# A hybrid retention and SSD block: two buffers for the tile of decays, six instead of seven for the weights' high parts

## The chip, the cores and the metric

The kernel runs on one core of a Trainium2 chip. The metric is the device time of one execution in microseconds (us). A difference below 0.2% of the time, about 5.5 us here, cannot be told from no change.

## The reference

One layer of a streaming encoder on 512 positions, model width 2048, all in float32:

```python
h = rmsnorm(x, norm1_w)
proj = einsum('bsd,de->bse', h, w_in)            # 2048 -> 22592 columns
q, k, v, g_ret, z, xbc, dt_raw, gate_r, gate_s = split(proj)
y_r = retention(q, k, v, positions) * silu(g_ret)      # 8 heads x 256, rotary, group norm
y_s = ssd(xbc, dt_raw, ...)                            # 64 heads x 64, state 128, chunked scan
y_s = rmsnorm(y_s * silu(z), ssd_norm_w)
merged = sigmoid(gate_r) * (y_r @ w_br_ret) + sigmoid(gate_s) * (y_s @ w_br_ssd)
x = rmsnorm(x + merged @ w_out, norm_f_w)
```

In the SSD branch each head has a scalar decay per position. Inside a chunk, the output is `(C B^T * decay) x`, where `decay[l, s] = exp(acum[l] - acum[s])` for `l >= s`. The tile of decays that this document is about holds these exponentials.

## The kernel before

**Units.** Every projection is cut into units of 256 output columns. A unit multiplies eight slices of 256 input rows (k = 0 to 7) with its weights. It uses Strassen's scheme with seven products for most units (`SEVEN`) and plain products for some (`FOUR`). Each product is three matmuls, since weights and operands are split into a high part and a low part of reduced precision: L202 (weights' high part times operands' high part), L203 (high times low) and L204 (low times high). The results stand in four PSUM banks, `pb0` to `pb3`.

**The weights' path.** For a pair of k, SP loads the weights into `wf` (L216, `FB` = 3 buffers). DVE forms the Strassen sums in place (L219, L221, L222). Then `split` makes the two parts for each k: ACT casts `wf` into `whi` (L150, `HB` = 7 buffers), and DVE subtracts that from `wf` into `wlo` (L151, `LB` = 6 buffers). A buffer of `whi` comes free after the last L203 that reads it, one of `wlo` after the last L204. The products of k = 0 to 4 are issued k by k, those of the last three k bank by bank, so the last three `whi` and `wlo` are held until a unit's end. After a unit its banks are evicted: L255 on ACT and L256 to L259 on DVE (L250 to L252 for plain units).

**The stages.** Retention (8 heads of four units), SSD (8 groups), the two branch projections, and the output projection. A group of SSD has a unit for B and C; then twice a unit for x, a unit for z and the work on two blocks of 128 features (a block is two heads); and units of the merge gates between them.

**A feature block.** SP loads the cumulated decays into `L` (L642, 512 KB, from a tensor in DRAM). ACT makes eight Relu steps of 128x128 (L646) and one Exp of 128x1024 (L648, ahead of which a table load stands when the last function was of another table, as SiLU and sigmoid are). DVE multiplies the result by `CB` (L649). PE then multiplies with it (L653, eight in the program, of which the trace shows sixteen). `L` had one buffer: the next block's load waits until the L653 of this block are done. Beside this runs the state's part: transposes (L620), `xd` on DVE (L622), `xl` on POOL (L625), L629 on PE, `S` on ACT and DVE (L632, L636), and L657 on PE. L659 to L662 on DVE put the block's output together.

**The order.** The program is written in the order of the code, and the framework's scheduler sets each engine's order from it, by priorities and by what its own model of the time says is ready. Each engine, and SP's queue of loads, then works strictly in that order. Another number of buffers gives another order on every engine.

Of the kernel before, what the change touches and what calls it, by code (L numbers as in the profile page):

```python
# [8 lines left out]
F32 = mybir.dt.float32  # L9
# [7 lines left out]
P = 128  # L17
T = 512
TB = T // P
# [80 lines left out]
          (((2, 0, 1, 6), (2, 0, 3, 2), (2, 1, 0, 6), (2, 1, 2, 2)),))  # L100
NP = KD // 2
LAST = 3
FB, HB, LB = 3, 7, 6
FORM_POOL = (1, 2, 3, 4, 5, 6, 7)
X_POOL = (2, 3, 4, 5, 6, 7)
PLAIN2 = (0, 7)
# [23 lines left out]
def hybrid_block(tc, A, out):  # L130
# [15 lines left out]
    def att_tile():  # L146
        return att.tile([P, T], F32, name="att")
# [409 lines left out]
    with tc.tile_pool(name="ssd", bufs=1) as sp:  # L557
# [30 lines left out]
        for g in range(NG):  # L588
# [14 lines left out]
            for jj in range(2):  # L603
# [5 lines left out]
                for e in range(2):  # L609
                    j = j0 + e  # L610
                    h0 = 2 * j
                    hs = slice(h0, h0 + 2)
                    y = xs[e]
                    E = sp.tile([P, T - P], F32, name="E")
                    for i in range(2):
                        SP.dma_start(out=E[i * 64:(i + 1) * 64, :], in_=E_d[h0 + i, P:].partition_broadcast(64))

                    ps = att_tile()
                    for c in range(TB):
                        PE.transpose(ps[:, c * P:(c + 1) * P], y[:, c * P:(c + 1) * P], ident)  # L620
                    xd = sp.tile([P, TB, 2, 64], F32, name="xd")
                    DVE.tensor_tensor(xd, ps.rearrange("p (c i d) -> p c i d", c=TB, i=2),  # L622
                                      dt[:, :, hs, None].to_broadcast([P, TB, 2, 64]), op=ALU.mult)
                    xl = sp.tile([P, TB - 1, 2, 64], F32, name="xl")
                    POOL.tensor_tensor(xl, xd[:, :TB - 1], tail[:, :TB - 1, hs, None].to_broadcast([P, TB - 1, 2, 64]),  # L625
                                       op=ALU.mult)
                    ps = att_tile()
                    for c in range(TB - 1):
                        PE.matmul(ps[:, c * P:(c + 1) * P], Bk[:, c, :], xl[:, c].rearrange("p i d -> p (i d)"),  # L629
                                  start=True, stop=True)  # L630
                    S = sp.tile([P, TB - 1, P], F32, name="S")
                    ACT.copy(S[:, 0, :], ps[:, :P])  # L632
                    for c in range(1, TB - 1):
                        for i in range(2):
                            d = slice(i * 64, (i + 1) * 64)
                            DVE.scalar_tensor_tensor(S[:, c, d], S[:, c - 1, d], cd[:, c, h0 + i:h0 + i + 1],  # L636
                                                     ps[:, c * P + i * 64:c * P + (i + 1) * 64],
                                                     op0=ALU.mult, op1=ALU.add)
                    pi = att_tile()

                    L = sp.tile([P, 2, TB, P], F32, name="L")
                    SP.dma_start(out=L.rearrange("p i c l -> p i (c l)"),  # L642
                                 in_=A_d[hs, :].partition_broadcast(P))
                    for i in range(2):
                        for c in range(TB):
                            ACT.activation(L[:, i, c, :], L[:, i, c, :], AF.Relu, scale=-1.0,  # L646
                                           bias=At[:, c, h0 + i:h0 + i + 1])
                    ACT.activation(L, L, AF.Exp, scale=-1.0)  # L648
                    DVE.tensor_tensor(L, L, CB[:, None].to_broadcast([P, 2, TB, P]), op=ALU.mult)  # L649

                    for c in range(TB):
                        for i in range(2):
                            PE.matmul(pi[i * 64:(i + 1) * 64, c * P:(c + 1) * P], xd[:, c, i, :], L[:, i, c, :],  # L653
                                      start=True, stop=True)
                    pe = att_tile()
                    for c in range(1, TB):
                        PE.matmul(pe[:, c * P:(c + 1) * P], S[:, c - 1, :], Ct[:, c * P:(c + 1) * P],  # L657
                                  start=True, stop=True)
                    DVE.scalar_tensor_tensor(y, y, dsk[:, j:j + 1], pi, op0=ALU.mult, op1=ALU.add)  # L659
                    DVE.tensor_tensor(E, pe[:, P:], E, op=ALU.mult)  # L660
                    DVE.tensor_tensor(y[:, P:], y[:, P:], E, op=ALU.add)
                    DVE.tensor_tensor(y, y, sz[e], op=ALU.mult)  # L662
                    if j == 0:
                        ACT.activation(sq, y, AF.Square)
                    else:
                        ACT.activation(sz[e], y, AF.Square)
                        POOL.tensor_tensor(sq, sq, sz[e], op=ALU.add)
                    ACT.activation(y, y, AF.Identity, scale=sn[:, j:j + 1])
                    ACT.dma_start(out=ys_d[j * P:(j + 1) * P, :], in_=y)
# [155 lines left out]
```

## Time and profile before

| | |
|---|---|
| median of 3 runs | 2768.67 us (2764.48 to 2770.89) |
| the profiled execution's own time | 2775.27 us |
| its span, first to last instruction | 2772.7 us, granted TensorE clock 0.992 |
| PE busy | 2701.6 us (97%) |
| DVE busy | 2389.5 us (86%) |
| ACT busy | 1343.8 us (48%) |
| retention / SSD / what follows | about 0 to 808, 808 to 2040, 2040 to 2773 us |

Busy time is counted by engine; PE counts matmuls, PEld the loading of their stationary operand, which overlaps. A wait is named as "engine and line that waited <- engine and line that ended the wait: us in total, times, longest us". Each engine waits in its own order, so a wait also holds back all that stands behind the instruction.

### The profile page before, as it was taken

To read this page: it belongs to the slowest core of one execution; us is meant where nothing else is said; L and a number is where in the kernel's file an instruction comes from. 1 tells how busy PE (TensorE), PEld (TensorE's weight loads), DVE (VectorE), ACT (ScalarE), POOL (GpSimd) and SP (SyncE) were. 2 spreads that over 40 slices of the span, in tenths; PEclk is the share of its full clock that TensorE was granted. 3 is DMA by queue.
4 is the path that set the end of the run, shared out by engine and by line. 5 is a ranking of instruction groups with operands and counts; after the bars stand their busy time and mean duration, and the time that the engine had idled before them with its cause. 6 is when DMAs were issued, how large, how long until landed. Compare 5 with 4: busy or idle time off the path is not lost.

```text
span 2772.7 us, 52195 instructions
## 1 busy us (share of the span) xinstructions
PE 2701.6 (97%) x20508; PEld 2567.9 (93%) x20508; DVE 2389.5 (86%) x3750; ACT 1343.8 (48%) x1884; POOL 268.3 (10%) x206
## 2 busy tenths in 40 slices
PE   7999999999999999999999999999999999999898
PEld 3899999999999999999999999999979989899798
DVE  8998888888869888988889899898989797888997
ACT  4344333333345565555565565565553343433453
POOL 4000000000000000000000000000020020121321
PEclk9999999999999999999999999999999999999999
DMA  3333333333333444343344434344365454556634
GB/s 125 99 103 103 97 111 104 103 92 103 103 112 120 128 128 129 113 125 122 123 128 130 133 115 126 117 126 130 125 193 167 157 186 136 165 184 198 218 113 137
DMA packets 339765, 362.46 MB, mean 131 GB/s; under 512 B 25152, under 2 KB 297792, under 8 KB 339520
## 3 DMA queue, kind: packets, MB, share of 16 engines
q1 hardware_dynamic: 319280, 325.31, 38.5%
q10 hardware_dynamic: 20240, 33.82, 3.3%
q8 instruction: 160, 2.62, 0.4%
q14 instruction: 85, 0.70, 0.1%
HBM read 321.56 MB, written 37.49 MB: 129 GB/s over the span
## 4 chain that ended last, share of the span: by engine, by line
PE 79%; DVE 10%; DMA 5%; issue 3%; POOL 1%; ACT 1%; SPq 1%; DVEq 0%; POOLq 0%; ACTq 0%
PE pb L204 21%; PE pb L203 21%; PE pb L202 21%; DVE wlo L151 3%; PE att L202 3%; PE att L204 3%; PE att L203 3%; DMA wf<-in_w_in_dram 3%; PE att L536 1%; PE att L521 1%; PE att L653 1%; DVE wf L219 1%; DMA wf<-in_w_br_ssd_dram 1%; PE att L657 1%; PE pb L120 1%
## 5 line engine op out<-in xcount | busy, mean ns | idle before, releaser
L203 PE MATMUL pb<-hl,whi 128*128 128x256 f32 (+1 forms) x5464 | 1599.5, 294 | 12.9 <-DVE hl L120 8.5
L202 PE MATMUL pb<-hh,whi 128*128 128x256 f32 (+1 forms) x5464 | 1597.7, 295 | 14.5 <-ACT hh L150 7.8
L204 PE MATMUL pb<-hh,wlo 128*128 128x256 f32 (+1 forms) x5464 | 1589.2, 294 | 5.1 <-DVE wlo L151 5.0
L150 ACT CAST whi<-wf 128x896 fp32r<-128x896 f32 (+1 forms) x968 | 819.6, 886 | 913.6 <-PE pb L203 367.2
L202 PEld LDWEIGHTS pb<-hh,whi 128*128 128x128 f32 x5464 | 1045.2, 192 | 40.3 <-ACT hh L150 8.9
L203 PEld LDWEIGHTS pb<-hl,whi 128*128 128x128 f32 x5464 | 1047.9, 192 | 35.9 <-DVE hl L120 10.2
L204 PEld LDWEIGHTS pb<-hh,wlo 128*128 128x128 f32 x5464 | 1041.7, 192 | 28.2 <-DVE wlo L151 7.1
L151 DVE TENSOR_TENSOR wlo<-wf,whi 128x896 fp32r<-128x896 f32 (+1 forms) x968 | 1005.1, 1051 | 56.3 <-ACT whi L150 32.1
L219 DVE TENSOR_TENSOR wf<-wf 128x512 f32<-128x512 f32 x404 | 289.9, 718 | 176.9 <-DMA wf<-in_w_in_dram 133.2
L202 PE MATMUL att<-hh,whi 128*128 128x256 f32 (+1 forms) x768 | 227.1, 297 | 3.0 <-ACT whi L150 3.0
L203 PE MATMUL att<-hl,whi 128*128 128x256 f32 (+1 forms) x768 | 226.7, 297 | 0.0
L204 PE MATMUL att<-hh,wlo 128*128 128x256 f32 (+1 forms) x768 | 222.8, 297 | 2.1 <-DVE wlo L151 2.1
L222 DVE TENSOR_TENSOR wf<-wf 128x256 f32<-128x256 f32 x404 | 179.9, 446 | 3.2
L221 DVE TENSOR_TENSOR wf<-wf 128x256 f32<-128x256 f32 x404 | 171.9, 426 | 3.5
L202 PEld LDWEIGHTS att<-hh,whi 128*128 128x128 f32 x768 | 147.4, 192 | 7.8 <-ACT whi L150 3.9
L204 PEld LDWEIGHTS att<-hh,wlo 128*128 128x128 f32 x768 | 144.8, 191 | 7.2 <-DVE wlo L151 3.1
L203 PEld LDWEIGHTS att<-hl,whi 128*128 128x128 f32 x768 | 147.5, 192 | 3.9
L625 POOL TENSOR_TENSOR xl<-xd,sst 128x384 f32<-128x384 f32 x32 | 35.1, 1097 | 848.7 <-DVE xd L622 791.1
L646 ACT ACTIVATE L<-L,sst 128x128 f32<-128x128 f32 x256 | 78.5, 389 | 29.7 <-DMA L<-A_d 29.7
L542 POOL TENSOR_TENSOR rs<-rs,mhalf 128x1 f32<-128x1 f32 x32 | 23.8, 750 | 712.9 <-DVE rs L541 678.8
L255 ACT COPY o<-pb 128x256 f32<-128x256 f32 x89 | 32.7, 367 | 117.9 <-PE pb L204 110.8
L256 DVE TENSOR_TENSOR o<-pb,o 128x512 f32<-128x512 f32 x89 | 60.8, 683 | 31.4 <-PE pb L204 30.8
(230 smaller groups left out, 2099.1 us busy)
## 6 DMA issues: line engine op xcount, KB each, us to landing
wf<-in_w_in_dram SPq DMA_DIRECT2D x640, 256.0 KB, 3.1
wf<-in_w_br_ssd_dram SPq DMA_DIRECT2D x128, 256.0 KB, 3.6
wf<-in_w_out_dram SPq DMA_DIRECT2D x72, 256.0 KB, 3.2
wf<-in_w_in_dram SPq DMA_DIRECT2D x128, 128.0 KB, 2.6
L<-A_d SPq DMA_DIRECT2D x32, 512.0 KB, 3.7
wf<-in_w_br_ret_dram SPq DMA_DIRECT2D x64, 256.0 KB, 3.5
ys_d<-B ACTq DMA_DIRECT2D x32, 256.0 KB, 2.2
E<-E_d SPq DMA_DIRECT2D x64, 96.0 KB, 3.4
```

Of the source, the lines that this page charges most:

```text
L150: ACT.copy(dst_hi, src)
L151: DVE.tensor_tensor(dst_lo, src, dst_hi.bitcast(F32), op=ALU.subtract)
L202: PE.matmul(o, wh, xh, start=b not in started, stop=False, skip_group_check=True)
L203: PE.matmul(o, wh, xl, start=False, stop=False, skip_group_check=True)
L204: PE.matmul(o, wl, xh, start=False, stop=(k == NP - 1), skip_group_check=True)
L219: DVE.tensor_tensor(f2[:, :, 4:6, :], f2[:, :, 1:3, :], f2[:, :, 0:1, :].to_broadcast([P, 2, 2, P]), op=ALU.subtract)
L221: DVE.tensor_tensor(f2[:, :, 0, :], f2[:, :, 2, :], f2[:, :, 4, :], op=ALU.add)
L222: DVE.tensor_tensor(f2[:, :, 6, :], f2[:, :, 3, :], f2[:, :, 0, :], op=ALU.subtract)
L255: ACT.copy(p1, pt[0][:, 0, :])
L256: DVE.tensor_tensor(o[:, 1:3, :], pt[1], p1[:, None, :].to_broadcast([P, 2, 256]), op=ALU.add)
L625: POOL.tensor_tensor(xl, xd[:, :TB - 1], tail[:, :TB - 1, hs, None].to_broadcast([P, TB - 1, 2, 64]), op=ALU.mult)
L646: ACT.activation(L[:, i, c, :], L[:, i, c, :], AF.Relu, scale=-1.0, bias=At[:, c, h0 + i:h0 + i + 1])
```

## The change

The pool of the decays' tile gets two buffers, and the pool of the weights' high parts loses one. Nothing is computed differently, and the instructions are the same but for the table loads that the new order needs (58 on ACT instead of 70: at L648 17 instead of 30, at L579 17 instead of 16).

```diff
-FB, HB, LB = 3, 7, 6
+FB, HB, LB = 3, 6, 6
...
-                    L = sp.tile([P, 2, TB, P], F32, name="L")
+                    L = sp.tile([P, 2, TB, P], F32, name="L", bufs=2)
                     SP.dma_start(out=L.rearrange("p i c l -> p i (c l)"),
                                  in_=A_d[hs, :].partition_broadcast(P))
```

The scheduler makes another order of this on every engine. Three places show it.

PE, SSD's fifth group, around the L653 of the first pair's second block, before (`pb_16478` to `pb_16480` are banks of the unit that runs beside it; `hh_266`, `hh_277`, `hh_288` are the operands of its k = 5, 6, 7):

```order
L202 MATMUL pb_16480<-hh_266,whi 128x256
L653 MATMUL att<-L,xd 64x128 x8
L657 MATMUL att<-A_8595,S 128x128 x2
L203 MATMUL pb_16480<-hl_284,whi 128x256
L204 MATMUL pb_16480<-hh_266,wlo 128x256
L202 MATMUL pb_16480<-hh_266,whi 128x256
L203 MATMUL pb_16480<-hl_284,whi 128x256
L204 MATMUL pb_16480<-hh_266,wlo 128x256
L202 MATMUL pb_16480<-hh_277,whi 128x256
L657 MATMUL att<-A_8595,S 128x128
```

The same place now:

```order
L202 MATMUL pb_16478<-hh_266,whi 128x256
L629 MATMUL att<-xl,A_8595 128x128 x3
L653 MATMUL att<-L,xd 64x128 x8
L203 MATMUL pb_16478<-hl_284,whi 128x256
L204 MATMUL pb_16478<-hh_266,wlo 128x256
L202 MATMUL pb_16477<-hh_277,whi 128x256
L203 MATMUL pb_16477<-hl_290,whi 128x256
L204 MATMUL pb_16477<-hh_277,wlo 128x256
L202 MATMUL pb_16478<-hh_277,whi 128x256
```

The second block's L653 moved up, to right behind its L629; its three L657 no longer stand close behind the L653 but further down, with products between them.

ACT, the same group, from the first pair's second block to the next block, before:

```order
L255 COPY o<-pb_16477 128x256
L669 DMA ys_d<-B_8596 128x512
L150 CAST whi<-wf 128x896 x3
L646 ACTIVATE L<-L,sst 128x128 x8
L584 ACT_TABLE_LOAD
L584 ACTIVATE o<-o 128x512 x2
L648 ACT_TABLE_LOAD
L648 ACTIVATE L<-L 128x1024
```

And now:

```order
L255 COPY o<-pb_16477 128x256
L646 ACTIVATE L<-L,sst 128x128 x8
L150 CAST whi<-wf 128x896
L648 ACTIVATE L<-L 128x1024
L150 CAST whi<-wf 128x896 x2
L584 ACT_TABLE_LOAD
L584 ACTIVATE o<-o 128x512 x2
```

The decays here are those of the next pair's first block before, and of the next pair's second block now; the Exp comes ahead of the gates' sigmoid (L584), and one table load of the two is gone.

ACT, retention's fifth head, around an eviction, before (`whi_5463` to `whi_5575` are k = 0 to 4 of the next unit):

```order
L150 CAST whi_5463<-wf_5457 128x896
L150 CAST whi_5488<-wf_5457 128x896
L150 CAST whi_5519<-wf_5513 128x896
L150 CAST whi_5544<-wf_5513 128x896
L255 COPY o_5383<-pb0_5155 128x256
L150 CAST whi_5575<-wf_5569 128x896
```

And now:

```order
L150 CAST whi_5463<-wf_5457 128x896
L150 CAST whi_5488<-wf_5457 128x896
L150 CAST whi_5519<-wf_5513 128x896
L255 COPY o_5383<-pb0_5155 128x256
L150 CAST whi_5544<-wf_5513 128x896
L150 CAST whi_5575<-wf_5569 128x896
```

The cast of the next unit's fourth k moved from ahead of the eviction to behind it.

## Prediction

> **What bounds the kernel now.** I read the page's first lines, then the busy time by stage, then the waits of TensorE in the stage that the change is about, and last the timeline there.
>
> ```profile
> span 2772.7 us, 52195 instructions
> PE 2701.6 (97%) x20508; PEld 2567.9 (93%) x20508; DVE 2389.5 (86%) x3750; ACT 1343.8 (48%) x1884; POOL 268.3 (10%) x206
> ```
>
> TensorE (PE) is the bound: 97% of the span, and 71 us of idle time in all. The number of matmuls doesn't change, so no gain can be larger than idle time that goes. The busy time by stage (columns: stretch, its length, PE, PEld, DVE, ACT and POOL busy, granted clock, DMA share, GB/s) says where it lies:
>
> ```profile
> 0.00:80.00 80.00, 57.91 (x170) 31.93 (x171) 69.05 (x92) 37.29 (x40) 30.27 (x26) 0.89 0.41 128
> 80.00:808.00 728.00, 727.23 (x5697) 705.83 (x5696) 617.64 (x1083) 280.87 (x363) 23.82 (x32) 1.00 0.33 101
> 808.00:2040.00 1232.00, 1218.72 (x9640) 1172.39 (x9639) 1066.61 (x1675) 717.91 (x1103) 85.43 (x62) 1.00 0.41 125
> 2040.00:2275.00 235.00, 228.06 (x1513) 208.97 (x1512) 204.87 (x291) 101.50 (x120) 38.81 (x33) 0.99 0.56 179
> 2435.00:2605.00 170.00, 154.92 (x1097) 144.43 (x1096) 153.60 (x219) 60.89 (x75) 44.40 (x26) 0.97 0.65 202
> 2605.00:2735.00 130.00, 130.00 (x1052) 128.40 (x1051) 120.03 (x165) 65.35 (x87) 28.00 (x15) 1.00 0.41 135
> ```
>
> The tile of decays exists only in SSD, from 808 to 2040. There PE idles 1232.00 - 1218.72 = 13.3 us, against 0.8 us in all of retention. The start idles 22.1 us, the stretch behind SSD 6.9 us, the last branch projection 15.1 us. So the second buffer of `L` plays for 13.3 us at the very most. DVE at 1066.61 of 1232 (87%) is the next bound, and the change takes no work from it.
>
> PE's waits from 808 to 2040 (what waited, what ended it, us in total, times, longest):
>
> ```profile
> PE pb L202 <- DVE o L258: 3.3, 5, 1.2
> PE att L657 <- DVE S L636: 2.9, 6, 1.2
> PE att L653 <- issue: 2.7, 5, 1.1
> PE pb L202 <- DVE o L256: 2.7, 4, 1.6
> PE att L599 <- ACT A L579: 1.2, 1, 1.2
> PE att L629 <- POOL xl L625: 0.3, 1, 0.3
> ```
>
> Together 13.1 us, which is the stage's idle time. One of the five waits of L653 in the timeline, with DVE ahead of it:
>
> ```profile
> 1560.84 1.21 DVE L649 TENSOR_TENSOR L<-L,A 128x1024 f32<-128x1024 f32 x1
> 1562.15 1.09 PE L653 MATMUL att<-L,xd 128*64 128x128 f32 x16 [1.10 <-issue]
> ```
>
> L649 ends at 1562.05 and L653 starts at 1562.15: what the view calls issue is the decays coming late. So 2.7 us is the price, seen on PE, of the single buffer.
>
> **The change, part by part.** *The second buffer of L.* With one buffer the load of a block's decays starts when the last block's L653 are done, and stands in SP's queue until then; ACT waits for its landing.
>
> ```profile
> SPq L642 <- PE att L653: 76.6, 29, 5.5
> L<-A_d SPq DMA_DIRECT2D x32, 512.0 KB, 3.7
> L646 ACT ACTIVATE L<-L,sst 128x128 f32<-128x128 f32 x256 | 78.5, 389 | 29.7 <-DMA L<-A_d 29.7
> ```
>
> With two, the scheduler has the decays of a pair's first block and its second ready a whole block earlier: in PE's order L653 stands right behind its L629. By the rows, load to landing, eight Relu, Exp and L649 make a chain of about 3.7 + 2.5 + 1.1 + 1.2 us, and this chain no longer lies between two L653. **The 2.7 us go: -2.7** (bounds -2.7 and 0). What is late next at that place is L629 itself, for which PE now waits 0.3 us.
>
> *The three L657.* They wait for `S`, which ACT (L632) and DVE (L636) make behind L629: 2.9 us in six waits. In the new order nine to twenty products stand between L653 and the later L657, where one to six stood. But `S` of the second block now stands in ACT's queue behind the next decays' Exp and its table load (1.06 + 1.28 us, below), so a part may stay. Bounds -2.9 and +2.9 (as much again); I take **-1.2**, somewhat under half of a removal, since both reasons are real.
>
> *The evictions.* PE starts a unit only on banks that DVE has emptied: 3.3 + 2.7 = 6.0 us. They follow stretches in which ACT was busy with the decays:
>
> ```profile
> 1498.91 2.46 ACT L646 ACTIVATE L<-L,sst 128x128 f32<-128x128 f32 x8 [0.54 <-DMA L<-A_d]
> 1501.39 1.28 ACT L584 ACT_TABLE_LOAD   x1
> 1502.68 1.15 ACT L584 ACTIVATE o<-o 128x512 f32<-128x512 f32 x2
> 1503.85 1.28 ACT L648 ACT_TABLE_LOAD   x1
> 1505.15 1.06 ACT L648 ACTIVATE L<-L 128x1024 f32<-128x1024 f32 x1
> 1506.11 0.62 ACT L666 ACTIVATE B<-B 128x512 f32<-128x512 f32 x1
> 1506.76 0.72 ACT L668 ACTIVATE B<-B,sn 128x512 f32<-128x512 f32 x1
> 1507.39 0.92 ACT L150 CAST whi<-wf 128x896 fp32r<-128x896 f32 x1
> ```
>
> For 8.5 us no weight is cast; the splits, the loads of `wf` behind them and the evictions in DVE's queue all come later for it. In the new order this run is cut by casts and has one table load less. A late cast is then no longer the reason; DVE's amount of work still is. Bounds -6.0 and +6.0; I take half of a removal, **-3.0**.
>
> *The table loads.* Twelve fewer by the order, at 1283 ns from this row:
>
> ```profile
> L648 ACT ACT_TABLE_LOAD x30 | 38.5, 1283 | 0.5
> ```
>
> That is 15.4 us off ACT, which is busy 717.91 of 1232 us in SSD: ACT has idle time beside it, so 0 in the sum except through the evictions above. The Trainium skill ("ScalarE: Activation LUTs", What ACT_TABLE_LOAD costs) gives 1283 ns for the load and about 1380 ns more for a drain, 2.66 us for each switch. By it twelve switches would free 31.9 us of ACT, still beside its idle time. The trace agrees with the load and shows no such drain: the load at 1501.39 ends at 1502.67 and the sigmoid starts at 1502.68.
>
> *Six buffers of whi.* Over the whole run, in the groups by line and the waits, PE waits for the splits as little as this, and ACT for free buffers that much:
>
> ```profile
> L204 PE MATMUL pb<-hh,wlo 128*128 128x256 f32 (+1 forms) x5464 | 1589.2, 294 | 5.1 <-DVE wlo L151 5.0
> L150 ACT CAST whi<-wf 128x896 fp32r<-128x896 f32 (+1 forms) x968 | 819.6, 886 | 913.6 <-PE pb L203 367.2 <-DVE wf L222 333.3 <-PE pb L204 67.8
> DVE wlo L151 <- PE pb L204: 13.9, 18, 1.6
> ```
>
> ACT runs ahead until the seventh buffer is full. But `wlo` has only six already, so a product's low part cannot start before the product six places back is done; the seventh buffer only lets the cast be over by then. Without it the cast comes in front of the subtraction: at most 0.886 us later, where the buffer was what DVE waited for. That is shown for 18 of 968 splits; fully exposed, 18 x 0.886 = 16.0 us. Against it stands that in retention, where buffers are fullest, PE lost 0.8 us in 728, so splits are done well before their use. The cast that moved behind an eviction does that eviction good. Bounds 0 and +16.0; near the row of 0.8 us, I take **+1.0**.
>
> *The start.* The order moves one split on DVE behind the low part of the fifth operand:
>
> ```profile
> 54.41 1.77 DVE L151 TENSOR_TENSOR wlo<-wf,whi 128x512 fp32r<-128x512 f32 x1
> 57.04 2.01 DVE L120 TENSOR_TENSOR hl<-B,hh 128x1792 fp32r<-128x1792 f32 x1
> 59.68 0.94 DVE L120 TENSOR_TENSOR A<-A 128x256 f32<-128x256 f32 x1 [0.62 <-POOL A L120]
> 59.11 0.80 PE L203 MATMUL pb<-hl,whi 128*128 128x512 f32 x1 [3.12 <-DVE hl L120]
> ```
>
> PE's wait of 3.12 us becomes 1.77 us shorter, but the next low parts are not moved, so PE waits there instead. Only DVE's own wait of 0.62 us for POOL is filled by the split that moved: **-0.6** (bounds -1.8 and 0).
>
> *Behind SSD.* The first operand of the next stage is loaded into SSD's buffers, and waited for the last L657; PE then waited for low parts:
>
> ```profile
> SPq L185 <- PE att L657: 5.8, 1, 5.8
> PE pb L203 <- DVE hl L151: 3.2, 4, 1.2
> ```
>
> The last block's L653 and L657 come a few products earlier, so this load does too. Bounds -3.2 and +3.2; the queue's order there changes in more places than I can price, so I take **-0.5**. The last branch projection, bound by DVE (153.60 of 170.00) and loads, is reordered without a direction: 0, with a fifth of its 15.1 us of idle time, 3, to both sides.
>
> The sum: -2.7 - 1.2 - 3.0 + 1.0 - 0.6 - 0.5 = **-7.0 us**. The profiled execution took 2775.27 us (its span 2772.7), so it would take 2768.3. The median of the runs shown, 2768.67, lies 6.6 us below it; the same 7.0 us from the median give **2762 us**.
>
> **The rivals.** *No change to be told.* Evictions and `S` are made by DVE, 87% busy in SSD with the same work as before; a wait that is removed at one place appears at the next. Then only L653 and the start are left: -2.7 - 0.6 = -3.3, some 2765 us. For it speaks that DVE's waits cause 8.9 of the 13.1 us; against it, that the chain of the decays was what disturbed DVE's order.
>
> *Slower.* The casts behind evictions make the split of a unit's fourth product late. There are 968 / 8 = 121 units. The mechanism decides once PE reaches the fourth product less than one cast, 0.886 us, after its `wlo` is done. If that holds in one unit of seven, 17 x 0.886 = 15.1 us; less 3.3 for L653 and the start, +11.8: 2780 us. In one unit of ten it is +7.3, 2776 us, which I take as its price. Against it stand the single wait of 0.8 us in retention and ACT's 367.2 us of waiting with all buffers full; for it, DVE's load in SSD.
>
> *A larger gain.* PEld is 1172.39 / 1232 = 95.2% busy in SSD, and 128.40 / 130 = 98.8% in the stretch from 2605. If the better order brought SSD to the same share, it would take 1172.39 / 0.988 = 1186.6 us: -45, some 2723 us. The Trainium skill's rule for this is in "Perfetto Trace Analysis", Identifying the Most-Contended Engine: headroom of TensorE is judged by the share of LDWEIGHTS, not of matmuls. Against it here: PE's waits name only 13.1 us, and SSD's small matmuls have other shares.
>
> **How the numbers follow.** The forecast, 2762 us, has a chance of 0.52, no change 0.30, slower 0.15, the larger gain 0.03. A measurement tells 0.2% or 5.5 us from no change, so faster gets 0.52 + 0.03 = 0.55, same 0.30, slower 0.15. The range's lower end takes all of SSD's 13.1 us, 1.8 of the start and 3.2 behind SSD less the 1.0: 17.1, so 2752. Its upper end reaches most of the way to the slower rival: 2773.
>
> **What would show it.** Right: no wait of L653 on `issue` (2.7 before), L657 and the evictions together at some 4 to 5 us where they had 8.9, SSD's idle time near 6.5 us, 17 table loads at L648, and retention's idle time still under 2 us. Wrong: PE waits for `wlo` (L204 <- L151) in retention or SSD by more than 5 us in all, which is the slower rival; or the evictions keep their 6.0 us, which is the second. An error outside of these would be the stages behind 2040 us, if their new order moves their 22 us of idle time by more than I allow.

## Result: slower, by 0.6%

The changed kernel takes 2788.45 us in the median of four runs (2780.80 to 2791.61), the kernel before 2769.78 beside it; the ratio is 1.0061, 95% interval 1.0045 to 1.0078. The forecast was 2762 us, and its range ended at 2773. The profiled execution took 2789.62 us:

```profile
span 2787.5 us, 52135 instructions
PE 2708.5 (97%) x20508; PEld 2576.3 (92%) x20508; DVE 2381.5 (85%) x3750; ACT 1331.3 (48%) x1872; POOL 269.7 (10%) x206
```

The busy time by stage, with the columns of before:

```profile
80.00:808.00 728.00, 727.68 (x5701) 706.30 (x5700) 621.67 (x1082) 282.23 (x364) 22.35 (x32) 1.00 0.33 101
808.00:2040.00 1232.00, 1211.55 (x9519) 1164.48 (x9518) 1043.95 (x1656) 699.90 (x1082) 94.31 (x60) 0.99 0.41 124
2040.00:2275.00 235.00, 230.88 (x1550) 212.32 (x1549) 204.32 (x294) 105.40 (x126) 38.55 (x34) 0.99 0.56 178
```

Retention is untouched: 0.3 us of idle time. Its last L536 (a matmul of the attention) starts at 802.2 us (801.6 before). The last L657 starts at 2049.5 (2036.9), the last matmul of all at 2775.5 (2760.7). So of 14.8 us, 0.6 come up to the end of retention, 12.0 in SSD and 2.2 behind it. The medians lie further apart, 18.7 us; only the two profiled executions can be taken apart by rows.

PE's waits from 808 to 2040:

```profile
PE att L657 <- ACT S L632: 9.0, 9, 2.5
PE pb L202 <- DVE o L258: 3.1, 6, 1.0
PE pb L202 <- DVE o L252: 2.1, 1, 2.1
PE att L629 <- POOL xl L625: 1.8, 3, 1.4
PE pb L202 <- DVE o L256: 1.2, 2, 0.8
PE att L657 <- DVE S L636: 1.0, 3, 0.6
PE pb L202 <- DVE o L259: 1.0, 2, 0.5
PE pb L204 <- DVE wlo L151: 0.5, 1, 0.5
```

They sum to 19.7 us, against 13.1. L653's wait is gone; the three L657 wait 10.0 us instead of 2.9, nearly all of it for ACT's copy `S`, which caused no wait worth a row before. Where ACT was meanwhile shows in its group for L646 (instructions with their busy time and mean, then the idle time ahead of them and what ended it):

```profile
L646 ACT ACTIVATE L<-L,sst 128x128 f32<-128x128 f32 x256 | 78.7, 389 | 67.7 <-DMA L<-A_d 67.6
L<-A_d SPq DMA_DIRECT2D x32, 512.0 KB, 4.9
```

ACT stands 67.6 us in waits for the load of `L`, where it stood 29.7. The load is issued earlier, in the median of the 32 blocks 68 us ahead of the block's first L653 instead of 22. But ACT asks for it earlier by as much: it has finished what stands ahead of the Relu 2.8 us after the issue, where that was 2.7. The load itself now takes 4.9 us in the median instead of 3.7. From these medians, 32 x (4.9 - 2.8) = 67 us against 32 x (3.7 - 2.7) = 32: an estimate that comes near both waits, so they grew with the load. Why the load takes longer, no run isolates. The timeline of the longest stall, around a pair's second block:

```profile
1645.87 1.10 PE L653 MATMUL att<-L,xd 128*64 128x128 f32 x16
1649.26 0.46 SPq L642 DMA_DIRECT2D L<-A_d  x1
1654.55 0.83 PE L629 MATMUL att<-xl,A 128*128 128x128 f32 x6
1655.72 2.45 ACT L646 ACTIVATE L<-L,sst 128x128 f32<-128x128 f32 x8 [3.67 <-DMA L<-A_d]
1658.07 0.92 ACT L150 CAST whi<-wf 128x896 fp32r<-128x896 f32 x1
1659.02 1.28 ACT L648 ACT_TABLE_LOAD   x1
1660.31 1.06 ACT L648 ACTIVATE L<-L 128x1024 f32<-128x1024 f32 x1
1661.27 0.25 ACT L632 COPY S<-att 128x128 f32<-128x128 f32 x1
1661.57 0.79 PE L657 MATMUL att<-A,S 128*128 128x128 f32 x2 [2.46 <-ACT S L632]
```

The first block's L653 free a buffer at 1646.97. SP issues the next pair's load at 1649.26, and ACT waits for it from 1652.05 to 1655.72. Those decays are needed by an L653 at 1716.5, 60 us later. The copy that L657 needs now has its input at 1655.4 and stands behind the eight Relu, a cast, a table load and the Exp until 1661.27. ACT could not go round them.

After the stall the clock falls (columns as in the stages above; the granted clock stands behind POOL's count):

```profile
1658.90:1661.50 2.60, 0.21 (x2) 0.01 (x1) 1.86 (x3) 2.57 (x5) 0.00 (x0) 1.00 0.74 250
1661.57:1664.98 3.41, 3.41 (x16) 3.41 (x17) 3.41 (x6) 2.98 (x8) 1.63 (x1) 0.50 0.23 87
1664.98:1668.00 3.02, 3.02 (x27) 3.02 (x27) 2.67 (x7) 2.54 (x6) 0.00 (x0) 1.00 0.00 0
```

For 3.41 us PE is granted half its clock, which costs it up to 1.7 us of work. SSD has four such stretches in this execution, each behind a wait of 1.8 to 2.5 us (three of L657 for `S`, one of L202 for the eviction at L252), and none before. So the 12.0 us are 6.6 us of waits and up to 6.8 us of half clock, less what was won elsewhere. In the other three runs the mean clock was 0.992 to 0.993, as before, and they took 2780.80 to 2791.61 us: the half clock is not needed for the loss. What those runs lost in its place, no trace shows.

### The profile page after: what moved, and what is told of

It is laid out like the page before. It is cut to its first block, busy times and chain, and to the rows that moved or that the text cites. A ratio compares the mean times of both kernels' runs of the same rounds, so it can differ in the third digit from the quotient of the medians.

```text
span 2787.5 us, 52135 instructions
## 1 busy us (share of the span) xinstructions
PE 2708.5 (97%) x20508; PEld 2576.3 (92%) x20508; DVE 2381.5 (85%) x3750; ACT 1331.3 (48%) x1872; POOL 269.7 (10%) x206
## 4 chain that ended last, share of the span: by engine, by line
PE 67%; DVE 13%; DMA 10%; issue 5%; ACT 2%; SPq 1%; POOL 1%; DVEq 0%; ACTq 0%; POOLq 0%
PE pb L203 19%; PE pb L204 19%; PE pb L202 19%; DMA wf<-in_w_in_dram 4%; DVE wlo L151 4%; PE att L202 2%; PE att L203 2%; PE att L204 2%; DMA wf<-in_w_br_ssd_dram 2%; DVE wf L219 1%; PE att L536 1%; PE att L521 1%; SPq L216 1%; PE pb L120 1%; ACT L L646 1%
## 5 line engine op out<-in xcount | busy, mean ns | idle before, releaser
L202 PE MATMUL pb<-hh,whi 128*128 128x256 f32 (+1 forms) x5464 | 1597.4, 296 | 16.4 <-ACT hh L150 5.9
L202 PEld LDWEIGHTS pb<-hh,whi 128*128 128x128 f32 x5464 | 1048.0, 192 | 41.7 <-ACT hh L150 6.9
L202 PE MATMUL att<-hh,whi 128*128 128x256 f32 (+1 forms) x768 | 226.6, 297 | 0.0
L222 DVE TENSOR_TENSOR wf<-wf 128x256 f32<-128x256 f32 x404 | 173.8, 431 | 2.7
L221 DVE TENSOR_TENSOR wf<-wf 128x256 f32<-128x256 f32 x404 | 172.0, 427 | 2.3
L202 PEld LDWEIGHTS att<-hh,whi 128*128 128x128 f32 x768 | 147.8, 193 | 4.0
L625 POOL TENSOR_TENSOR xl<-xd,sst 128x384 f32<-128x384 f32 x32 | 41.4, 1293 | 879.1 <-DVE xd L622 879.1
L646 ACT ACTIVATE L<-L,sst 128x128 f32<-128x128 f32 x256 | 78.7, 389 | 67.7 <-DMA L<-A_d 67.6
L667 POOL TENSOR_TENSOR R<-R,B 128x512 f32<-128x512 f32 x31 | 56.4, 1818 | 273.4 <-ACT B L666 273.4
```

Of the source, the lines that this page charges most:

```text
L202: PE.matmul(o, wh, xh, start=b not in started, stop=False, skip_group_check=True)
L221: DVE.tensor_tensor(f2[:, :, 0, :], f2[:, :, 2, :], f2[:, :, 4, :], op=ALU.add)
L222: DVE.tensor_tensor(f2[:, :, 6, :], f2[:, :, 3, :], f2[:, :, 0, :], op=ALU.subtract)
```

## The experiments

Theory Q, formed on these rows: the second buffer lets the scheduler put the next pair's decays ahead of the second block's `S` on ACT, and ACT stands there in a wait for their load. Rivals: B, the missing seventh `whi`; N, the nearness of L629 and L657 in PE's new order; M, many small delays on DVE. Ratios are to the kernel before, run beside each. "PE waits" is the sum of the rows of PE's waits from 808 to 2040.

| run | ratio (95% interval) | PE waits, us |
|---|---|---|
| before | 1 | 13.1 |
| changed | 1.0061 (1.0045 to 1.0078) | 19.7 |
| six whi, one L | 0.9991 (0.9981 to 1.0000) | 5.6 |
| changed, S on DVE | 1.0043 (1.0031 to 1.0054) | 18.1 |
| before, S on DVE | 0.9996 (0.9987 to 1.0005) | 7.4 |
| changed, Relu behind the last S | 1.0072 (1.0059 to 1.0085) | 27.5 |
| the same, xl on DVE | 0.9959 (0.9946 to 0.9972) | 1.3 |
| changed, xl on DVE | 1.0024 (1.0015 to 1.0033) | 14.4 |
| six whi, one L, xl on DVE | 1.0021 (1.0012 to 1.0030) | 11.0 |
| changed, L loaded from ACT's queue | 1.0096 (1.0079 to 1.0113) | 23.7 |
| changed, Relu behind the last L653 | 0.9980 (0.9971 to 0.9990) | 4.8 |
| the same, xl on DVE | 0.9985 (0.9976 to 0.9995) | 4.0 |
| changed, first blocks held | 1.0041 (1.0026 to 1.0057) | 18.5 |
| changed, second blocks held | 1.0015 (1.0003 to 1.0028) | 11.1 |
| changed, no load of L | 0.9996 (0.9988 to 1.0005) | 9.6 |
| six whi, one L, no load of L | 1.0030 (1.0019 to 1.0041) | 12.7 |

**One half of the change: six `whi`, one `L`.**

```diff
-FB, HB, LB = 3, 7, 6
+FB, HB, LB = 3, 6, 6
```

> Only the half of the change that takes a buffer of whi away: six of them, and L with one buffer as before. Theory Q (queue order): with the second L, ACT waits for the next pair's decays ahead of the copy S that TensorE needs now, and TensorE's stalls of 2.0 to 2.6 us are each followed by 3.4 us of half clock; six whi buffers cost next to nothing. It expects no wait of L657 on ACT's S above 1.5 us, none of the four half-clock stretches in SSD, and 2765 to 2775 us, so -5 to +5 against before. Theory B (buffers): the missing seventh whi makes the splits late; the second L is harmless. It expects 2780 us or more, +10 to +19 against before. Theory M (many small delays in DVE's queue from the new order): anything between, with TensorE's waits on evictions above the 6.0 us of before.

It is as fast as before or a little faster, so theory B falls: the loss comes only with the second `L`. (Two `L` with seven `whi` was not run.)

**`S` on VectorE**, in the changed kernel and, as a control, in the one before.

```diff
-                    ACT.copy(S[:, 0, :], ps[:, :P])
+                    DVE.tensor_copy(S[:, 0, :], ps[:, :P])
```

> The changed kernel, both halves kept, but the copy of S (L632, 128x128) made by VectorE instead of ScalarE, so that it no longer stands behind the wait for the next decays. Theory Q: TensorE's 9.0 us of L657 waiting for ACT's S go, VectorE's S may keep 1 to 4 us, the half-clock stretches behind them go, and the time falls by 10 to 20 us from the changed kernel: -6 to +3 against before. Theory B: the buffers are the same, so nothing of the loss comes back, +12 to +19 against before. Theory M: 32 copies of about 0.3 us more on VectorE (some 10 us of work) make the evictions later still: +15 to +25.

> A control for the run above: the kernel before (seven whi, one L) with the copy of S made by VectorE. TensorE waited for ACT's S not at all there and 2.9 us for VectorE's part. Theory Q: nothing to win, -2 to +5 against before. If it is faster by the same 10 to 20 us as the same edit gives the changed kernel, then the edit is good in itself and shows nothing on the queue order (theory Q weakened).

The control gains nothing. The changed kernel comes to 1.0043, which its interval does not tell from 1.0061, and lies 10 us above before, where theory Q expected 3 at most. The wait moved from ACT's copy to DVE:

```profile
PE att L657 <- DVE S L636: 10.6, 12, 1.7
```

The rows are half a hit: the longest of these waits fell from 2.5 to 1.7 us, and SSD's half-clock stretches from four to one, but their sum did not fall. The timeline at 1657 us shows why:

```profile
1652.99 2.45 ACT L646 ACTIVATE L<-L,sst 128x128 f32<-128x128 f32 x8 [2.79 <-DMA L<-A_d]
1655.34 0.92 ACT L150 CAST whi<-wf 128x896 fp32r<-128x896 f32 x1
1656.30 1.09 DVE L151 TENSOR_TENSOR wlo<-wf,whi 128x896 fp32r<-128x896 f32 x1 [1.02 <-ACT whi L150]
1657.31 0.28 DVE L632 COPY S<-att 128x128 f32<-128x128 f32 x1
```

DVE stands ahead of `S` in a wait for ACT's cast, and that cast stands behind ACT's wait for `L`. The copy left ACT's queue, but still hangs on it.

**The order of ACT fixed.** The eight Relu of a block come behind the copy of `S` of the block before; no work is added. (Line numbers rise by 1 up to the Relu and by 6 or 7 behind it: L600 is L599, L626 is L625, L630 is L629, L633 is L632, L637 is L636, L643 is L642, L647 is L646, L656 is L649, L664 is L657, L667 is L660.)

```diff
+                            if last_copy[0] is not None:
+                                tc.add_manual_dep(r, last_copy[0], NoSync, ...)
```

> The changed kernel, both halves kept and all work on its engine, with one order fixed: the eight Relu of a block's decays may stand on ScalarE only behind the copy of S of the block before. Theory Q: the wait of L657 on ACT's S falls from 9.0 us to 3 us or less with none over 1.5 us, no half-clock stretch in SSD comes from it, and the time falls by 8 to 18 us from the changed kernel: -5 to +6 against before; L653 may wait again for up to 2.7 us. Theory B: +12 to +19 as in the changed kernel. Theory M: between, since the order on VectorE changes only a little.

The first part came as expected: PE waits for ACT's `S` no longer, ACT for `L` 3.0 us. The time did not, since another link gave way:

```profile
PE att L630 <- POOL xl L626: 18.3, 6, 3.4
PE att L664 <- DVE S L637: 2.9, 3, 1.1
```

```profile
1725.34 4.68 POOL L626 TENSOR_TENSOR xl<-xd,sst 128x384 f32<-128x384 f32 x1 [8.49 <-DVE xd L623]
1726.51 1.23 DVE L656 TENSOR_TENSOR L<-L,A 128x1024 f32<-128x1024 f32 x1
1727.64 0.69 DVE L219 TENSOR_TENSOR wf<-wf 128x512 f32<-128x512 f32 x1
1728.25 1.09 DVE L151 TENSOR_TENSOR wlo<-wf,whi 128x896 fp32r<-128x896 f32 x1
1729.25 0.56 DVE L667 TENSOR_TENSOR E<-att,E 128x384 f32<-128x384 f32 x1
1730.08 0.38 PE L630 MATMUL att<-xl,A 128*128 128x128 f32 x1 [3.30 <-POOL xl L626]
```

The same multiplication on POOL takes 0.83 us elsewhere in this execution; here, and at four other places, it takes 4.68, while DVE runs one step with two inputs in SBUF after another without a gap. The Trainium skill ("SBUF — State Buffer", Who interferes with whom) says that a DVE instruction with two SBUF inputs contends with a GpSimd instruction that reads SBUF, and that the lock on what they share is exclusive. The rows agree: POOL's step ends at 1730.02, 0.77 us after DVE has come to L667, one input of which (`att`) lies in PSUM. The 3.85 us more are over three times DVE's longest step, 1.23, so POOL lost several turns in a row, not one.

**The same with `xl` on DVE, and that edit alone.**

```diff
-                    POOL.tensor_tensor(xl, xd[:, :TB - 1], ...
+                    DVE.tensor_tensor(xl, xd[:, :TB - 1], ...
```

> The run with the Relu behind the copy of S, plus one edit: xl (L625 there L626) made by VectorE instead of GpSimd. In that run the copy of S was in time, but xl took 4.68 us on GpSimd six times instead of 0.83, with VectorE busy all through, and TensorE waited 18.3 us for it. If that is what ate its gain: the wait on xl falls to under 3 us, the half-clock stretches behind it go, and the time falls by 12 to 24 us to -6 to +6 against before, as theory Q had expected of the run without this edit. Theory N: VectorE has 32 more steps of some 0.6 us (19 us of work) in the same close chain, xl and S are waited for by turns, and +8 to +18 stays.

> The changed kernel with xl on VectorE and no order fixed: what of the gain of the run with both edits (0.9959 of before) is due to xl alone. Theory Q: the load of L is still waited for on ScalarE ahead of the second block's S, and +6 to +19 stays. If xl on GpSimd was the whole cause: -15 to -5.

> A control and a candidate: six whi, one L (which was as fast as before), with xl made by VectorE. xl took 1.48 us in the mean there against 0.83 at best, and TensorE waited 1.0 us for it. If the edit is good in itself it is -8 to -2 against before; if VectorE's 19 us of added work show in the evictions, +2 to +10. Only if this run is no faster can a gain of the run above be put down to its chain.

With both edits the kernel is the fastest of all, 2755.32 us in the median, and beats both kernels of the case: 13 us under before, more than the 6 expected at best. All that PE waits for in SSD is

```profile
PE att L600 <- ACT A L579: 0.8, 1, 0.8
PE pb L202 <- DVE o L251: 0.5, 1, 0.5
```

The order alone gave 1.0072. `xl` alone gave 1.0024, +6.6 us and so at the low end of what was expected: it takes back more than half of the loss though ACT still waits 40.6 us for `L`, and L657 waits 1.9 us for ACT's `S` there instead of 9.0. Only together do the two edits give 0.9959. With one `L`, `xl` on DVE made the kernel slower, 1.0021: the edit is not good in itself. In the fastest kernel the first L657 stands 11 to 18 of the unit's matmuls behind L629, hardly further than in the changed kernel (mostly 11 to 21; the expectations call these matmuls products), and waits for nothing. That is against theory N: nearness is no loss once ACT and `xl` are in time.

**The load of `L` from ACT's queue.**

```diff
-                    SP.dma_start(out=L...
+                    ACT.dma_start(out=L...
```

> The changed kernel with one edit: the load of L is issued from ScalarE's queue instead of SP's. TensorE's order stays the same to within a few products, and ScalarE still works on the next pair's decays ahead of the second block's S. In the changed kernel that load was issued 2.3 us after its buffer came free and took 6 us, behind loads of wf in SP's queue. Theory Q (ScalarE stands in a wait for that load while TensorE needs S): the wait for L falls from 67.6 us by half or more, L657's wait for ACT's S from 9.0 to under 4 us, three of the four half-clock stretches in SSD go, and the time falls by 6 to 14 us: 0 to +11 against before. Theory N (nearness: the new order brings the steps xl, L629, S, L657 of the second block within 11 to 21 products on TensorE, where 48 stood; whatever is slowest in that chain then shows): the wait moves to VectorE's S or to xl, and the time falls by less than 5 us: +12 to +19.

It missed its aim, and the time, 24 us above before, is more than either theory expected. The load took 5.0 us in the median on the other queue too, and ACT's wait for it rose:

```profile
ACT L L646 <- DMA L<-A_d: 77.6, 28, 4.3
PE att L657 <- DVE S L636: 10.4, 7, 2.4
PE pb L202 <- DVE o L258: 9.6, 11, 1.9
```

So it says nothing on an earlier load; it shows that with the wait the loss stays.

**The old order with two buffers.** The Relu of a block come behind the L653 of the block before, as one buffer would have had it, and only the load runs ahead.

```diff
+                            if last_mm[0] is not None:
+                                tc.add_manual_dep(r, last_mm[0], NoSync, ...)
```

> The changed kernel, two buffers of L, but the eight Relu of a block are set in ScalarE's order behind the L653 of the block before, as one buffer would have set them; only the load runs ahead. L657 then stands 26 to 30 products behind L629 in both blocks of a pair, instead of 11 and 11 to 21. Theory N: waits of L657 fall from 10.0 to under 4 us and the half-clock stretches go: -5 to +5 against before. Theory Q: the second block's S still stands behind the next decays' eight Relu (2.45 us), but these no longer wait for a load, so the wait falls as well: -5 to +6. What tells them apart is the row: if L657 still waits for ACT's S by 5 us or more though no load is waited for, the order on ScalarE alone is enough for the loss, and neither theory's nearness or load is needed.

```profile
PE att L664 <- DVE S L637: 3.6, 7, 0.9
PE pb L202 <- DVE o L251: 0.5, 1, 0.5
PE pb L202 <- DVE o L258: 0.4, 1, 0.4
ACT L L647 <- DMA L<-A_d: 2.1, 1, 2.1
```

The same buffers, 0.9980: 22 us less than the changed kernel by the ratios (0.0081 of 2768). No L653 waits, ACT's wait for the load is 2.1 us, and no stretch of SSD has half clock. ACT still has the next decays' Relu (2.45 us) ahead of the second block's `S`, without harm. The evictions, which theory M blamed, take 0.9 us. So the loss lay in the order made of the buffers, not in the buffers. Against six `whi` and one `L` (0.9991) no gain of the second `L` is clear, since the intervals overlap. Nor does this run tell theory Q from theory N, as the first L657 stands mostly 26 to 30 matmuls behind L629 in it. With `xl` on DVE besides, the held order measures 0.9985, 4.5 us under before: two gains that add were expected to give 10 to 18, so they do not add.

**Only one block of a pair held**, the first or the second (`if e == 0 and ...`, `if e == 1 and ...` in the edit above).

> The changed kernel with the Relu held behind the L653 of the block before for the first block of each pair alone: the decays of the next pair no longer go ahead of the second block's S on ScalarE's queue, those of a pair's second block stand as in the changed kernel. Theory Q puts the loss there: ScalarE's wait for L falls from 67.6 us to under 40, L657's wait for ACT's S from 9.0 to under 3 us, at most one half-clock stretch is left in SSD, and the time is -6 to +4 against before. If the second block's decays are as much to blame: +6 to +12.

> The other half: the Relu held for the second block of each pair alone; the next pair's decays still go ahead of the second block's S. Theory Q: the wait for ACT's S stays at 5 us or more with stalls of 2 us and half-clock stretches behind them, +8 to +19 against before. If holding back either half is enough: -5 to +5.

Both went against theory Q. Holding the first blocks removes ACT's `S` from PE's waits, as it said, but the time, 1.0041, is not told from 1.0061 by the intervals. Holding the second ones removes three quarters of the loss, and ACT's `S` from PE's waits too, though the next pair's decays still stand ahead of the second block's `S`. In the pair around 1640 us they run from 1639.66 to 1643.91, and `S` follows at 1645.24, in time for L657 at 1646.92. So the place in the order does harm only where ACT comes to it late; ACT's wait for `L` is 19.0 and 21.3 us in these two runs, of 67.6. What is left of the first is a third form of the same chain:

```profile
1411.37 0.65 DVE L637 SCALAR_TENSOR_TENSOR S<-S,sst,att 128x64 f32<-128x64 f32 x3
1414.00 0.69 DVE L219 TENSOR_TENSOR wf<-wf 128x512 f32<-128x512 f32 x1 [1.97 <-DMA wf<-in_w_in_dram]
1414.61 0.28 DVE L637 SCALAR_TENSOR_TENSOR S<-S,sst,att 128x64 f32<-128x64 f32 x1
1414.94 0.38 PE L664 MATMUL att<-A,S 128*128 128x128 f32 x1 [1.58 <-DVE S L637]
```

Three of the four steps of `S` are done; DVE then stands 1.97 us in a wait for weights, with the fourth step (0.28 us) behind it and PE waiting for that. Theory Q was too narrow: not one copy, but whichever step of `xl`, L629, `S` stands behind an instruction that waits.

**The load left out**, with two `L` and with one: the Relu read a constant tile, so the decays are others.

```diff
-                    SP.dma_start(out=L.rearrange("p i c l -> p i (c l)"), ...
-                            ACT.activation(L[:, i, c, :], L[:, i, c, :], AF.Relu, ...
+                            ACT.activation(L[:, i, c, :], tri, AF.Relu, ...
```

> The changed kernel with the load of L left out: the eight Relu read the constant triangle that is in SBUF anyway, so the decays are not the reference's; everything else runs as in the changed kernel, and ScalarE still has the next pair's Relu, table load and Exp ahead of the second block's S. If standing in the wait for the load is what costs (theory Q as I first had it): L657's wait for S falls under 4 us, no half-clock stretch from it, and the time comes to -12 to 0 against before. If the order alone costs (the 4.8 us of Relu, table load and Exp ahead of S, casts and splits): L657's wait stays at 5 us or more, and +4 to +15 stays.

> The control for the run above: six whi, one L, and the load of L left out in the same way. It has 16 MB less to load, as the run above. If it is as fast as that run to within 4 us, then without the load the second buffer costs nothing, and the load is a necessary part of the loss; if it is faster by 6 us or more, the second buffer's order costs without any load. I expect -10 to +1 against before.

With two buffers and no load, 0.9996, though ACT has Relu, table load and Exp ahead of the second block's `S` as before. PE's waits have no row of `S`:

```profile
PE att L629 <- POOL xl L625: 4.1, 3, 2.3
PE pb L202 <- DVE o L258: 2.0, 3, 1.4
PE pb L204 <- DVE wlo L151: 1.5, 4, 0.6
```

With the load the second buffer cost 0.70% (1.0061 against 0.9991); without it, it gains 0.34% (0.9996 against 1.0030). So the loss needs the load, which fits theory Q: the eager order does harm where ACT stands in a wait in it. That the run with one buffer got slower without its load, by 0.4%, I had not expected and did not pursue. It also warns of how much any new order by itself moves this kernel, and the scheduler made new orders in these two runs as well.

## Why the prediction was wrong

- **The three L657, -1.2 (bounds 2.9 either way): the step that failed.** It measured +7.1 (2.9 to 10.0). The prediction saw that `S` would stand behind the next decays' Exp and table load on ACT, and priced that at "as much again" as the wait of before. It did not ask whether those decays would have landed. The row for it was quoted there: ACT waits 29.7 us for `L`. It was read as a wait that goes, since the load starts earlier; but the order took the decays earlier by as much, the load took 4.9 us instead of 3.7, and the wait became 67.6. What an engine that waits holds back (`S`, casts, through them DVE) was left at nothing, since ACT is idle half the time.
- **The half clock** had no term. In the profiled execution it is up to 6.8 us in SSD, and up to 3.4 us in two more stretches at 2477 and 2498 us that the execution before does not have.
- **L653, -2.7:** right, the row is gone. **Table loads:** 17 at L648, as the order said; no row shows a worth of them.
- **The evictions, -3.0:** wrong in sign; 6.0 became 7.4 (3.1 + 2.1 + 1.2 + 1.0). They seem to follow not ACT's time with the decays but ACT's lateness, which grew: DVE waits 51.0 us for ACT's casts in SSD, where it waited 27.9. No run isolates this.
- **Six `whi`, +1.0:** rightly near nothing, if not of that sign. Retention idles 0.3 us, and the half of the change with six `whi` alone measures -0.09% with an interval that ends at zero.
- **The start and the end, -0.6 and -0.5:** +0.6 up to the end of retention and +2.2 behind SSD; no run isolates either.
- **The rivals.** The slower one had the side but not the mechanism: PE waits 0.5 us for `wlo` in SSD, and six `whi` are harmless. The rival of no change had a part of it: a wait that went at L653 came back at L657, but larger. The range left out the true case because its upper end, 2773, was set short of the slower rival's price of 2776. The upper bounds of the terms themselves add up to +31.1 us (2.9 + 6.0 + 16.0 + 3.2 + 3), most of it for the six `whi`, where the loss was not; the bound of the three L657, +2.9, came from a wait that was there before. The larger gain, 2723 us, no run came near: the fastest takes 2755.32, with PEld 96.3% busy in SSD (1185.97 of 1232), where it is 94.5% here.

## What to carry to other kernels

When another buffer lets a scheduler move work up, ask of each instruction that it moves whether its input will have landed there, and what is queued behind it on that in-order engine; an engine that is busy half the time is not free while it waits. A buffer and the order made of it are separate edits: pinning the order (here a dependency that only the scheduler sees and that adds no instruction) can keep the early load and drop the harm. When a pinned order doesn't pay, look for the next link of the same chain, and fix both before judging either.

## What the runs showed of the hardware

- The points at which PE's granted clock changes lie on a grid of 3.41 us in every trace. Laid on this grid, from 808 to 2045 us of all sixteen traces, each of the sixteen steps of the grid in which PE was idle for 1.83 us or more was followed by half clock, and none of some 5800 others at full clock, with up to 1.76 us. So it matters how an idle time falls on the grid, not only how long it is. The four of the changed kernel (1.83 to 2.46 us) lay whole in one step. Waits of 2.26 and 2.25 us in the two runs without the load, and of 2.14 us with `xl` alone on DVE, were cut by a point of the grid into at most 1.76 us, and the clock stayed. Outside this stretch of time the border is less sharp, between 1.7 and 1.85 us. The Trainium skill ("TensorE: Matmul & The Clock Gate", What's actually happening) has the clock fall after a whole idle window of some 3.4 us. The length of the slow stretches agrees with that window; the idle time ahead of them is shorter than it.
- A POOL multiplication of 128x384 took between 0.83 and 4.68 us, the longest of them beside five DVE steps in a row with two inputs in SBUF; on DVE it took 0.55.
